# First pair of cached sequences compressed one sequence at a time in a hybrid attention decoder step

## Chip, cores and metric

The kernel runs on one core of one Trainium2 chip. The metric is the device time of one execution in microseconds; of several runs the median counts.

## The reference, cut to what matters

The program is one step of a one-layer decoder: adaLN conditioning, one input projection, forgetting attention beside native sparse attention, a gated merge, an output projection and an MLP. The change lies in the first stage, where the raw keys and values of eight cached sequences (2048 tokens each, in pages of 128 tokens that a page table names) are compressed. What is computed there:

```python
def compress_blocks(x, pos, w1, w2):
    b, n = x.shape[:2]
    n_chunk = n // CMP_STRIDE                        # 16
    xc = x[:, :n_chunk * CMP_STRIDE].reshape(b, n_chunk, CMP_STRIDE, NSA_GROUPS, HEAD_DIM)
    ...
    lead = jnp.einsum('bncgd,cdh->bngh', xc + pos[0], w1[0])
    trail = jnp.einsum('bncgd,cdh->bngh', xc + pos[1], w1[1])
    return jnp.einsum('bngh,hd->bngd', jax.nn.silu(lead[:, :-1] + trail[:, 1:]), w2)

nsa_all = jnp.concatenate([gather_pages(nsa_pool, page_table), pm['nsa_rows']], axis=1)
kc, vc, c_end = compressed_kv(nsa_all[:, :, 0], nsa_all[:, :, 1], lp)
mod = jnp.einsum('bd,de->be', jax.nn.silu(c), lp['w_ada']) + lp['b_ada']
h = rms_norm(x, lp['norm1_g']) * (1.0 + sc1) + sh1
```

The conditioning `mod` and the first norm of the 576 new tokens are worked on in the same stage, between the units of the compression.

## The kernel before

**First stage.** Sequences are handled in four pairs. A unit `u` of 32 is one pair (`u // 8`), one group `j` of four taps (`u // 2 % 4`) and k or v (`u % 2`). For each unit there are these steps:

- `cmp_order` (line 115 is the copy): VectorE copies a tap group of each sequence's pages, tile `cpg`, into a tile `ro` of 128 x 1024; three `ro` buffers exist.
- `cmp_taps`, for the first eight units: ScalarE rounds the tap weights `w1rawk`, `w1rawv` to a high part (line 112) and VectorE makes the low part (line 131), into `w1hlk`, `w1hlv`.
- `rows_turn`: TensorE transposes `ro` into a PSUM bank `ct` (line 83), four transposes for each sequence, one bank each, two banks in turn; ScalarE and VectorE split each bank in two steps each into `xh` and `xl`, a ring of two.
- `cmp_hidden`: twelve matmuls of 512 columns (line 77) add into the bank `hid` of k or v.

After eight units of a pair come `cmp_act` (tiles `csx`, `cst`), `cmp_out` (`co`) and `cmp_keys` (`kct`). Other work hangs in lists `todo[u]` behind the units: `ada_silu` and the turned conditioning, the bias (`posb`), the norms of five token tiles (`norm`, then `turned`, tile `nt`), eight products with `w_ada` (tile `ada`), a gather of log forget values (`lfg`), and loads.

**Order.** In this stage the order on TensorE is the order of the program, by a chain of dependencies (`link`). Order on ScalarE and VectorE is chosen by a planner that simulates a timeline; `issue_after(i)` puts the instructions of a block behind instruction `i` in the queue of its engine. `dma` chains the transfers of one issuing engine in program order.

**Loads.** Each page is one transfer of 128 KB with its page number in a register; each of the two `w1` loads of k or v is 512 KB. SyncE's queue carries nearly all: sequence 0 (16 pages), half of sequence 1, sequence 2, a tile of x, half of sequence 3, x, the conditioning vectors, eight small constants, the rest of sequence 3, w2, and then sequences 4 to 7, x and w_ada. ScalarE issues the `w1` loads of k, eight pages of sequence 1 and the `w1` loads of v. The planner was told to place the constants for later stages (`late_constants`) behind unit 8.

**Afterwards** the projection (`z`), prompt attention, sample attention, merge and MLP follow; the change does not touch them.

Of the kernel before, what the change touches and what calls it, by code (L numbers as in the profile page):

```python
# [14 lines left out]
P = 128  # L15
# [30 lines left out]
class Step:  # L46
# [165 lines left out]
    def constants(self):  # L212
# [4 lines left out]
        for i, n in enumerate("kv"):  # L217
            self.dma("sync", pos[16 * i:16 * i + 16], I[f"cmp_pos_{n}"].rearrange("o (j c) d -> (o j) (c d)", c=2))
        self.dma("sync", c("ptT", [P, 1], I32), I["page_table"].rearrange("b (n o) -> (b n) o", o=1))
        self.dma("sync", chan[0:48], I["b_ada"].rearrange("o (j p) -> (o j) p", p=P))  # L220
        self.dma("sync", chan[48:56], I["norm1_g"].rearrange("o (j p) -> (o j) p", p=P))
        self.dma("sync", chan[56:64], I["norm2_g"].rearrange("o (j p) -> (o j) p", p=P))
        for i, n in enumerate(["fox_qn_g", "nsa_qn_g", "nsa_kn_cmp_g"]):
            self.dma("sync", gains[i:i + 1].rearrange("o (a d) -> o a d", a=2),
                                dram(I[n], 0, [[64, 1], [0, 2], [1, 64]]))
# [13 lines left out]
    def late_constants(self):  # L239
# [14 lines left out]
        for i, n in enumerate(["fox_kn_g", "nsa_kn_slc_g", "nsa_kn_win_g"]):  # L254
            self.dma("sync", kgain[:, i, :], dram(I[n], 0, [[0, P], [1, 64]]))
        self.dma("sync", c("bfox", [P, 8]), dram(I["b_fox_f"], 0, [[0, P], [1, 8]]))
# [5 lines left out]
    def ada_start(self):  # L262
# [3 lines left out]
        self.dma("sync", c9[0:1], self.I["c_prompt"].rearrange("o (k c) -> o k c", k=NK))  # L266
        self.dma("sync", c9[1:9], self.I["c_sample"].rearrange("b (k c) -> b k c", k=NK))
# [83 lines left out]
    def cmp_weights(self, pl):  # L351
# [7 lines left out]
        for i in range(2):  # L359
            x = [pl.tile([P, 2, 514], F32R, name=f"x{n}{i}") for n in "hl"]  # L360
            for t in x:
                self.nc.vector.memset(t[:, :, 512:514].bitcast(F32), 0.0)
            self.ring.append(x)

    def cmp_taps(self, u):

        taps = lambda w: w.rearrange("p (a j) h -> p a j h", a=4)[:, :, u // 2]
        w = self.w1[u % 2]
        self.split(taps(w[:, 0]), taps(w[:, 1]), taps(self.w1raw[u % 2]))

    def cmp_second(self):

        self.w2 = []
        for n in "kv":
            w2 = self.keep.tile([P, 64], F32, name=f"w2{n}")
            w2r = self.keep.tile([P, 64], F32, name=f"w2raw{n}")
            self.dma("sync", w2r, self.I[f"cmp_w2_{n}"][0])
            self.ts(w2, w2r, 0.5, None, OP.mult)
            self.w2.append(w2)
# [57 lines left out]
    def cmp_order(self, pl, n):  # L437

        self.ros[n] = []
        for b in (2 * (n // 4), 2 * (n // 4) + 1):  # L440
            o = pl.tile([P, 2, 4, 2, 64], F32, tag="ro", bufs=3, name=f"ro{n}_{b}")
            self.cp(o.rearrange("p h x c d -> p h c x d"),
                    self.cpg[b][:, :, 2 * (n % 4):2 * (n % 4) + 2].rearrange("p h c (x d) -> p h c x d", x=4))
# [1691 lines left out]
```

## Time and profile before

| | |
|---|---|
| three runs | 1268.05, 1271.83, 1272.16 us; median 1271.83 |
| profiled execution | 1268.96 us, span 1267.2 us |
| granted TensorE clock, mean | 0.985 |
| TensorE busy in the span | 94% |
| DMA | 188.09 MB, mean 148 GB/s |
| first transpose of a page (`ct`) | 26.6 us |
| first matmul of `hid` | 35.6 us |
| last matmul of `hid` ends | 190.5 us |

The times of the rows are microseconds from the start of the span. A row of the timeline has start, length, engine, line, operation, output and inputs, count, and in brackets the engine's idle time before it with what ended it. A "q" behind an engine's name means its sequencer, which issues transfers. In the chain of work that ended last a row has start and length.

### The profile page before, as it was taken

What the parts mean: (1) busy time and instruction counts of PE and PEld (TensorE: products, weight loads), DVE (VectorE), ACT (ScalarE), POOL (GpSimd) and SP (SyncE); (2) the same over time, 40 slices, a digit from 0 to 9 for tenths busy, and PEclk for the clock granted to TensorE, in tenths of its full rate; (3) what the DMA queues carried; (4) which work ended last, traced back from release to release, by engine and by line L of the source; (5) the groups of instructions that cost most, each with busy time, mean ns of one, the idle gap of its engine ahead of it and who ended that gap; (6) DMA issues with size and microseconds to landing.
All of it is one profiled execution on the core that took longest, in us unless ns stands there. A gap on an engine that the chain in (4) does not pass through costs nothing.

```text
span 1267.2 us, 24533 instructions
## 1 busy us (share of the span) xinstructions
PE 1192.0 (94%) x9379; PEld 1021.6 (81%) x9379; DVE 707.1 (56%) x1904; ACT 502.4 (40%) x1119; POOL 99.5 (8%) x107
## 2 busy tenths in 40 slices
PE   0899999999999999999999998977999999999998
PEld 0777789999666656666799998977899899898997
DVE  2578676677688856556543434775234344344564
ACT  2344444444777854444432223233323132142230
POOL 0000000000221120000200000002011010010110
PEclk9899999999999999999999999988999999999999
DMA  9577528597695459796762333114223133141212
GB/s 207 167 225 186 166 66 272 180 332 236 184 297 174 111 199 319 243 316 225 167 175 76 85 99 104 31 50 120 65 83 109 44 115 94 40 133 54 81 34 75
DMA packets 177067, 188.09 MB, mean 148 GB/s; under 512 B 16901, under 2 KB 158766, under 8 KB 174774
## 3 DMA queue, kind: packets, MB, share of 16 engines
q1 hardware_dynamic: 168134, 178.13, 46.5%
q0 software_dynamic: 3504, 5.24, 1.6%
q10 hardware_dynamic: 5312, 3.15, 1.1%
q8 instruction: 74, 1.21, 0.4%
q14 instruction: 43, 0.35, 0.1%
HBM read 176.48 MB, written 30.90 MB: 164 GB/s over the span
## 4 chain that ended last, share of the span: by engine, by line
PE 84%; DVE 6%; DMA 4%; ACT 2%; SPq 2%; issue 1%; DVEq 0%; ACTq 0%
PE dn L77 16%; PE up L77 15%; PE z L77 9%; PE mg L77 8%; PE hid L77 5%; PE br L77 4%; PE wo L77 4%; PE ss L77 4%; PE k L83 2%; PE ct L83 2%; SPq L155 2%; PE so L77 2%; PE ada L77 2%; DMA cpg<-in_cache_nsa_kv 1%; PE sp L83 1%
## 5 line engine op out<-in xcount | busy, mean ns | idle before, releaser
L77 PE MATMUL dn<-wdh,u 128*128 128x512 f32 x576 | 181.9, 389 | 0.0
L77 PEld LDWEIGHTS dn<-wdh,u 128*128 128x128 f32 x576 | 107.5, 188 | 21.9
L77 PE MATMUL dn<-wdl,u 128*128 128x512 f32 x320 | 123.6, 389 | 0.0
L77 PE MATMUL z<-winh,h 128*128 128x264 f32 (+1 forms) x576 | 112.7, 289 | 1.9 <-DVE h L720 1.7
L77 PE MATMUL up<-h,wuh 128*128 128x256 f32 x512 | 94.4, 280 | 6.2 <-ACT h L112 6.2
L77 PEld LDWEIGHTS z<-winh,h 128*128 128x128 f32 x576 | 93.1, 192 | 4.0 <-DVE h L720 2.8
L112 ACT ACTIVATE wdh<-wdr 128x1024 fp32r<-128x1024 f32 x32 | 33.1, 1055 | 147.9 <-PE dn L77 127.6
L77 PE MATMUL z<-winl,h 128*128 128x264 f32 (+1 forms) x320 | 88.7, 286 | 0.0
L100 DVE TENSOR_TENSOR acc<-acc,dn 128x512 f32<-128x512 f32 x60 | 40.4, 686 | 86.3 <-PE dn L77 86.3
L131 DVE TENSOR_TENSOR wul<-wur,wuh 128x1024 fp32r<-128x1024 f32 x32 | 49.1, 1541 | 69.6 <-ACT wuh L112 69.6
L77 PEld LDWEIGHTS up<-h,wuh 128*128 128x128 f32 x512 | 81.2, 192 | 6.5 <-ACT h L112 6.5
L77 PE MATMUL up<-h3H,wuh 128*128 128x320 f32 x256 | 80.0, 313 | 5.8 <-ACT wuh L112 5.8
L77 PE MATMUL up<-h3H,wul 128*128 128x320 f32 x256 | 79.5, 311 | 0.3 <-DVE wul L131 0.3
L77 PE MATMUL up<-h3L,wuh 128*128 128x320 f32 x256 | 79.3, 310 | 0.0
L1926 POOL TENSOR_TENSOR u<-u 128x576 f32<-128x576 f32 x32 | 43.6, 1364 | 438.8 <-ACT u L112 433.6
L77 PE MATMUL mg<-hH,wmh 128*128 128x288 f32 x256 | 75.4, 296 | 1.1 <-ACT wmh L112 1.1
L77 PE MATMUL mg<-hH,wml 128*128 128x288 f32 x256 | 75.2, 295 | 0.9 <-DVE wml L131 0.9
L77 PE MATMUL mg<-hL,wmh 128*128 128x288 f32 x256 | 72.7, 295 | 0.0
L77 PE MATMUL up<-h,wul 128*128 128x256 f32 x256 | 71.7, 280 | 0.0
L112 ACT ACTIVATE xh<-ct 128x256 fp32r<-128x256 f32 x128 | 47.5, 385 | 57.9 <-PE ct L83 37.6
L83 PE MATMUL ct<-identF,ro 128*128 128x128 f32 x256 | 37.4, 292 | 35.1 <-DVE ro L115 30.2
L77 PEld LDWEIGHTS dn<-wdl,u 128*128 128x128 f32 x320 | 60.1, 188 | 12.5
(638 smaller groups left out, 2975.9 us busy)
## 6 DMA issues: line engine op xcount, KB each, us to landing
adw<-in_w_ada SPq DMA_DIRECT2D x16, 1024.0 KB
foxD<-in_cache_fox_kv SPq DMA_DIRECT2D x128, 128.0 KB
wur<-in_w_up SPq DMA_DIRECT2D x32, 512.0 KB
wdr<-in_w_down SPq DMA_DIRECT2D x32, 512.0 KB
cpg<-in_cache_nsa_kv SPq DMA_DIRECT2D x120, 128.0 KB
fr<-foxD SPq DMA_DIRECT2D x28, 512.0 KB
sr<-in_cache_nsa_kv SPq DMA_DIRECT2D x112, 128.0 KB
wada<-in_w_ada SPq DMA_DIRECT2D x8, 1024.0 KB
```

What stands on the lines that cost most here:

```text
L77: ins = self.nc.tensor.matmul(out, a, b, start=start, stop=stop, skip_group_check=True)
L83: ins = self.nc.tensor.transpose(out, in_, self.identF[:n, :n])
L100: self.nc.vector.tensor_tensor(out, a, b, op=op)
L112: return self.nc.scalar.activation(out, in_, f, **kw)
L131: self.splits.append((eng or self.nc.vector).tensor_tensor(l, x, h.bitcast(F32), op=OP.subtract).ins)
L155: self.issued[eng] = getattr(self.nc, eng).dma_start(out, in_).ins
L1926: nc.gpsimd.tensor_tensor(u[j], u[j], u[j], op=OP.mult)
```

## The change

- ScalarE's eight pages are those of sequence 0 (its second half); SyncE loads the other eight, then all of sequence 1, 2 and 3. A one-element Tanh on ScalarE at the start brings its table load there.
- The first two sequences are compressed by themselves: units 0 to 7 are sequence 0, units 8 to 15 sequence 1, both with 256 columns in `cmp_hidden` and one bank in `rows_turn`; units 16 to 39 are pairs 1 to 3 as before. All later work in `todo` moves by eight units.
- The small loads (constants, conditioning vectors) go to GpSimd's queue. Constants for later stages are no longer held back.
- In the first 16 units the copies of `cmp_order`, and the tap splits, are pinned right behind the splits of the unit before (`behind`). Norms start two units ahead of their transposes, not one; `ada_silu`, `stage_logf` and the halving of `w2`, now in place, are pinned too.

```diff
-        self.dma("sync", c("ptT", [P, 1], I32), I["page_table"].rearrange("b (n o) -> (b n) o", o=1))
+        self.dma("gpsimd", c("ptT", [P, 1], I32), I["page_table"].rearrange("b (n o) -> (b n) o", o=1))
...
-        self.dma("sync", c9[1:9], self.I["c_sample"].rearrange("b (k c) -> b k c", k=NK))
+        self.dma("gpsimd", c9[1:9], self.I["c_sample"].rearrange("b (k c) -> b k c", k=NK))
...
-                self.nc.vector.memset(t[:, :, 512:514].bitcast(F32), 0.0)
+                for c in (256, 512):
+                    self.nc.vector.memset(t[:, :, c:c + 2].bitcast(F32), 0.0)
...
     def rows_turn(self, u):
-        n, kv = u // 2, u % 2
+        _, bs, j, kv = self.units[u]
         xh, xl = self.ring[u % 2]
-        for s in range(2):
+        for b in bs:
+            s = b % 2
...
     def cmp_hidden(self, u):
+        c0, w = 256 * (bs[0] % 2), 256 * len(bs)
...
-            for w, x in three((wh, wl), self.ring[u % 2]):
-                self.mm(self.hid[i][kv], w[:, 4 * a + j, :], x[:, a % 2, a // 2:a // 2 + 512], n == 0, n == 47)
+            for y, x in three((wh, wl), self.ring[u % 2]):
+                self.mm(self.hid[i][kv][:, c0:c0 + w], y[:, 4 * a + j, :], x[:, a % 2, c0 + a // 2:c0 + a // 2 + w],
+                        n == 0, n == 47)
...
-        def late():
-            with self.tc.issue_after(self.splits[-1]):
-                self.late_constants()
+        def behind():
+            both = ExitStack()
+            for i in (self.last_high, self.splits[-1]):
+                both.enter_context(self.tc.issue_after(i))
+            return both
+
+        def pinned(f):
+            def g():
+                with behind():
+                    f()
+            return g
...
+        self.units = [(b // 2, bs, j, kv) for b, bs in ((0, (0,)), (1, (1,)), (2, (2, 3)), (4, (4, 5)), (6, (6, 7)))
+                      for j in range(4) for kv in range(2)]
...
-        self.cmp_pages("sync", 0)
-        self.cmp_pages("scalar", 1, slice(0, 8))
+        warm = self.small.tile([P, 1], F32, tag="warm", bufs=1, name="warm")
+        nc.vector.memset(warm, 0.0)
+        self.act(warm, warm, AF.Tanh)
+        self.cmp_pages("sync", 0, slice(0, 8))
+        self.cmp_pages("scalar", 0, slice(8, 16))
         self.cmp_raw(pe, 1)
-        self.cmp_pages("sync", 1, slice(8, 16))
+        self.cmp_pages("sync", 1)
         self.cmp_weights(pl)
+        self.ada_start()
+        self.constants()
+        self.late_constants()
         self.cmp_pages("sync", 2)
         load_x()
-        self.cmp_pages("sync", 3, slice(0, 8))
+        self.cmp_pages("sync", 3)
         load_x()
-        self.ada_start()
-        self.constants()
-        self.cmp_pages("sync", 3, slice(8, 16))
         self.cmp_second()
...
-        for k, u in enumerate((4, 6, 9, 11, 15)):
-            todo[u - 1] += [lambda k=k: norm(k)]
+        for k, u in enumerate((12, 14, 17, 19, 23)):
+            todo[u - 2] += [lambda k=k: norm(k)]
             todo[u] += [lambda k=k: turned(k)]
...
-        for u in range(32):
-            if u % 2 == 0 and u // 2 + 1 < 16:
-                self.cmp_order(pl, u // 2 + 1)
+        for u in range(40):
+            if u % 2 == 0 and u + 2 < 40 and u + 2 != 8:
+                with behind() if u + 2 < 16 else nullcontext():
+                    self.cmp_order(pl, u + 2)
             if u + 1 < 8:
-                self.cmp_taps(u + 1)
-            if u + 1 < 32:
+                with behind():
+                    self.cmp_taps(u + 1)
+            if u + 1 < 40:
                 self.rows_turn(u + 1)
+            if u + 2 == 8:
+                with behind():
+                    self.cmp_order(pl, u + 2)
             self.cmp_hidden(u)
```

86 lines of the change are left out of this document (46 added, 40 removed).

## The prediction

> **What bounds the kernel now.** The page comes first: engine shares, and the chain that ended last.
>
> ```profile
> span 1267.2 us, 24533 instructions
> PE 1192.0 (94%) x9379; PEld 1021.6 (81%) x9379; DVE 707.1 (56%) x1904; ACT 502.4 (40%) x1119; POOL 99.5 (8%) x107
> PE 84%; DVE 6%; DMA 4%; ACT 2%; SPq 2%; issue 1%; DVEq 0%; ACTq 0%
> ```
>
> TensorE is busy for 94% of the span and carries 84% of the chain. Where the other 6% lie the table of windows tells, asked by stage: before the first transpose, the units of the first pair (named below), the second pair up to its last, the rest of the stage, and all behind it. Columns: length, then busy time of PE, PEld, DVE, ACT and POOL with counts, clock, DMA share, GB/s.
>
> ```profile
> 0.00:25.85 25.85, 0.00 (x0) 0.00 (x0) 5.20 (x18) 5.67 (x9) 0.52 (x6) 1.00 1.02 218
> 25.85:77.75 51.90, 42.63 (x263) 35.38 (x264) 30.36 (x90) 18.85 (x46) 1.21 (x1) 0.93 0.58 168
> 77.75:120.10 42.35, 38.64 (x240) 30.61 (x238) 32.49 (x131) 20.76 (x50) 0.00 (x0) 0.96 0.84 223
> 120.10:190.47 70.37, 70.37 (x457) 55.85 (x457) 50.54 (x152) 32.17 (x79) 0.98 (x1) 1.00 0.39 120
> 190.47:1267.20 1076.73, 1040.37 (x8424) 899.75 (x8423) 588.53 (x1514) 425.01 (x938) 96.78 (x99) 0.99 0.47 145
> ```
>
> TensorE does nothing for 25.85 us, is idle for 9.3 of the next 51.9 and 3.7 of the next 42.35, and from 120 us to the end of the stage it is never idle. Everything the change touches lies in the first 190 us. Behind that the work is the same and hangs on TensorE, so what the stage ends earlier, the kernel ends earlier. The timeline shows what the early idle time waits for.
>
> ```profile
> 2.94 37.80 SPq L155 DMA_DIRECT2D cpg<-in_cache_nsa_kv  x40
> 14.52 1.28 ACT L112 ACT_TABLE_LOAD   x1 [14.52 <-DMA cpg<-in_cache_nsa_kv]
> 22.46 2.19 ACT L112 ACTIVATE w1hlv<-w1rawv 128x512 fp32r<-128x512 f32 x4 [4.46 <-DMA w1rawv<-in_cmp_w_v]
> 25.85 0.69 DVE L115 COPY ro<-cpg 128x1024 f32<-128x1024 f32 x1 [0.82 <-DMA cpg<-in_cache_nsa_kv]
> 30.58 1.30 DVE L115 COPY ro<-cpg 128x1024 f32<-128x1024 f32 x2 [1.11 <-DMA cpg<-in_cache_nsa_kv]
> 35.58 1.20 PE L77 MATMUL hid<-xh,w1hlk 128*128 128x512 f32 x2
> 52.12 1.05 ACT L112 ACTIVATE adw<-adw 9x1024 f32<-9x1024 f32 x1 [2.52 <-DMA adw<-in_c_sample]
> 55.03 1.94 PE L83 MATMUL ct<-identF,ro 128*128 128x128 f32 x8 [3.30 <-DVE xl L131]
> ```
>
> Sequence 0 is complete at 25.85 and sequence 1 at about 30.6; only then can the first pair's hidden product start, at 35.58. At 52 us ScalarE stands in front of the small load of c_sample, queued on SyncE behind 48 pages, and TensorE goes without work for 3.30 us.
>
> **The change, part by part.** A unit here is one tap group j of one of k and v for a pair: eight transposes, the splits, twelve matmuls. The first pair's 8 units become 16 of half the width.
>
> *Pages.* ScalarE's eight pages now belong to sequence 0, as SyncE's first eight do.
>
> ```profile
> L155 ACTq DMA_DIRECT2D cpg<-in_cache_nsa_kv x8: 546/546/671, 3.0 to 12.3; - x8
> 9.83 4.88 DMA cpg<-in_cache_nsa_kv
> 14.72 7.20 DMA cpg<-in_cache_nsa_kv
> ```
>
> The second kind of row is from the chain: 4.88 to 7.20 us from a page's issue to its landing. ScalarE issues its last page at 12.3, so sequence 0 is complete at 17.2 to 19.5. Counted in bytes, the 1 MB of k weights and 2 MB of pages take 14.5 us at 218 GB/s, which lies below that. I take 17.5, near the shorter lag since fewer pages are under way by then, 8.3 us earlier than now. Sequence 1's pages all come from SyncE; the bytes up to its end are the same, so about 30 us as now, when sequence 0 is not yet worked off. The fifteen small loads move from SyncE to GpSimd's queue, idle here; the nearest row prices an issue:
>
> ```profile
> 536.31 0.99 POOL L155 DMA_DIRECT2D hH<-hfd  x1 [76.56 <-DVE DH L100]
> ```
>
> That is 15 x 0.99 = 15 us of GpSimd, done by 20 us, needed from about 45 us on: nothing, unless they hold up the pages (0 to 1.5 us, my estimate for under 1,000 short packets over 16 engines). SyncE is rid of them, so pages 2 to 4 come no later. The early table load takes 1.28 us from ScalarE where it would otherwise issue or wait; it may delay its pages by up to 0.5 us and brings the first split forward.
>
> *Prices of a half unit.* First full clock, then the low one, then a product of near 256 columns (all from the chain), then the groups.
>
> ```profile
> 123.90 0.87 PE ct L83 x8
> 121.12 2.78 PE hid L77 x12
> 56.97 4.59 PE hid L77 x12
> 244.83 13.76 PE z L77 x112
> L131 DVE TENSOR_TENSOR xl<-ct,xh 128x256 fp32r<-128x256 f32 x128 | 50.2, 419 | 13.9 <-ACT xh L112 11.1
> L112 ACT ACTIVATE xh<-ct 128x256 fp32r<-128x256 f32 x128 | 47.5, 385 | 57.9 <-PE ct L83 37.6 <-DVE xl L131 18.0
> L115 DVE COPY ro<-cpg 128x1024 f32<-128x1024 f32 x32 | 21.1, 691 | 16.1 <-PE ct L83 14.0 <-DMA cpg<-in_cache_nsa_kv 1.9
> L131 DVE TENSOR_TENSOR w1hlv<-w1rawv,w1hlv 128x512 fp32r<-128x512 f32 x4 | 2.6, 686 | 4.2 <-ACT w1hlv L112 4.2
> ```
>
> A 264-column matmul is 13.76/112 = 0.123 us, so twelve of 256 are 1.43 us against half of 2.78 = 1.39: doubling the number of weight loads costs 16 x 0.04 = 0.6 us in all. With four transposes (0.44) a half unit is 1.87 us of TensorE at full clock and about 3.3 (half of 4.59, plus 1.0) at the low one. The split of a half unit is four steps in turn on one bank (ScalarE waits for VectorE and the other way round in the rows): 2 x (0.385 + 0.419) = 1.6 us. For sequence 0 VectorE also has the low half of the taps (0.69), now pinned between two units where all eight had been done before TensorE started, and every second unit a copy (0.69). In VectorE's order that makes 2.0 us a unit without and 2.7 with the copy, 2.4 in the mean, so sequence 0 runs at VectorE's pace, and sequence 1, without taps, at TensorE's.
>
> *The new course.* Copy at 17.5, transposes to 19.3, split to 21.0, product of unit 0 at the low clock to 23.6. Unit 1 needs the v weights, which ScalarE's queue still brings behind its pages, at 22.46: taps and split end at 25, product at 27.6. Unit 2, still slow, ends at 31, and five units of 2.4 us bring sequence 0 to 43. Ten slow microseconds are my choice after the rows: from 55.03 the clock stayed low to 60.81 (both windows stand under the first rival), and the units have gaps. The Trainium skill ("TensorE: Matmul & The Clock Gate", section Part 1: The HAM clock gate) gives about 3.4 us of sustained work before the full clock. By that rule one or two units less would be slow, at 3.3 - 1.87 = 1.4 us each, and the sum 1.4 to 2.8 us larger; the trace needed 5.8 us, the first half of them with stops, and I keep to it. Sequence 1 has 8 x 1.87 = 15 us of transposes and products, and the conditioning, bias and two norms that move in:
>
> ```profile
> 66.50 0.64 PE L83 MATMUL bc<-identF,adw 9*128 9x9 f32 x8
> 67.20 1.95 PE posb L77 x64
> 86.36 0.76 DVE x L104
> 53.21 1.21 DVE L109 SCALAR_TENSOR_TENSOR adw<-adw 9x1024 f32<-9x1024 f32 x1 [3.10 <-ACT adw L112]
> ```
>
> On TensorE that is 2.0 for the bias, about 1.2 for the small transposes and 2 x 0.87 for the norms': 20 us. On VectorE 16 x 0.42 + 4 x 0.69 + 1.2, two norms of some thirteen 0.16 us steps and 0.76, and four 0.69 us copies and products: 19 us. Both are close, so I add 3 us for hand-overs: 23, and sequence 1 ends at 66. Now the first pair ends at 77.75. **First part of the sum: -11.7 us** (ends: -16, at 19 us for sequence 1 and no loss at the start; -5, at 2.7 us a unit for sequence 0, pages at 19.5 and 26 us for sequence 1).
>
> *Behind the first pair.* The constants (small VectorE steps such as triU's below) leave the place, at 82 us, where they now stand in front of a norm, and norms start two units ahead instead of one.
>
> ```profile
> 82.37 0.22 DVE L104 TENSOR_SCALAR triU<-jp 128x128 f32<-128x128 int32 x1
> 88.27 1.86 PE ada L77 x16
> 100.95 1.00 PE ada L77 x16
> PE nt L83 <- DVE x L104: 3.7, 3, 2.0
> ```
>
> The last row is from TensorE's waits between 78 and 190 us (us in total, times, longest): 3.7 us, all of the idle time there. Behind the 2 us stop the clock is low for a while: 0.9 us on the sixteen ada matmuls, 1.86 against 1.00, and about as much, 0.8, on the eight transposes behind them. So 5.4 us are to be had; **I take -3**, since VectorE has the same norms to do (ends -5.4 and 0). *Edits with one answer.* The pins are an order in a queue and no new semaphore. On ScalarE silu stands behind unit 9's splits and in front of unit 10's; it waits for c_sample, which is there by 20 us, 25 us ahead: nothing. The gather of log forget values and its store keep their distance to the second pair, on GpSimd and SyncE. Four more small memsets run in VectorE's idle first microseconds, and halving w2 in place moves two small steps: nothing. w_ada's first loads go from unit 5 to 12 and 14, four half units ahead of their use, and on SyncE no longer stand behind the pages of sequence 5: nothing. From 120 us on TensorE is full now; the stage keeps its remaining work, and there is nothing to gain: 0. If the pages or w_ada came late for it, that would be the third rival.
>
> The sum is -11.7 - 3 = -14.7, say -14.5. The profiled execution took 1268.96 us, its span plus 1.8; it becomes 1254.5. It lies 2.9 below the median of 1271.83, which becomes 1257.3. I forecast **1256**.
>
> **The rivals.**
>
> *1. The thin units keep TensorE slow (slower).* At the low clock a half unit is 3.3 us; 16 of them, twice the 4.9 us of other products and the 3 us of hand-overs, from 21 us on, end at 21 + 53 + 10 + 3 = 87, 9 us behind the present 77.75; less the 3 us behind it, the kernel is 6 us slower: 1277. It decides at a mean of 2.9 us a unit, (77.75 + 3 - 21 - 10 - 3)/16, which the low clock passes and the full one does not. Here are stretches as long as the shortest one between two changes of the clock in the records (3.41 us):
>
> ```profile
> 53.98:57.40 3.42, 2.37 (x10) 2.31 (x11) 2.66 (x11) 1.49 (x4) 1.21 (x1) 0.50 0.18 40
> 57.40:60.81 3.41, 3.41 (x9) 2.64 (x9) 3.20 (x15) 0.82 (x3) 0.00 (x0) 0.50 0.60 194
> 337.29:340.70 3.41, 2.16 (x28) 1.46 (x26) 2.93 (x14) 2.22 (x7) 0.74 (x1) 1.00 0.75 202
> ```
>
> For it: a stretch 69% busy (53.98) did not lift the clock, one of 100% (57.40) did. Against it: at the low clock a half unit takes longer than VectorE's 2.4 us, so TensorE is full and the clock rises; once high, 63% busy (337.29) kept it, and my units are 78%. The Trainium skill has this rule ("TensorE: Matmul & The Clock Gate", section A second HAM failure mode: psum-queue depth-cycling): frequent short idle times between groups of matmuls can make the clock swing. The stretch at 337 us does not bear it out. Chance 0.05.
>
> *2. No overlap between half units (slower).* If transposes, split and product of a unit run one behind the other, a unit is 0.44 + 1.6 + 1.43 = 3.5, for sequence 0 with taps and copy 5.1: 18 + 41 + 28 + 5 = 92, 14 later, less 3: 1281. For it: the waits between ScalarE and VectorE above. Against it: the next transposes stand ahead of each product and two banks take turns. Chance 0.06.
>
> *3. The head start is given back.* Pages or w_ada for later pairs come when they came, TensorE waits, and the stage ends where it does: 1271, within 0.3%. Against it: the DMA engines moved 168 and 120 GB/s in two of the stretches above where 223 were reached in a third, and SyncE loses fifteen issues. Chance 0.07.
>
> *4. Pages are hardly earlier.* If GpSimd's short transfers and the weights hold sequence 0 until 23 to 25 us, about 6 us of the gain go: 1262. Nothing in the rows needs it beyond the 1.5 us above; the queues' shares of the engines are not shown. Chance 0.13.
>
> **How the numbers follow.** The forecast has 0.69, its own range -8 to -20: 1250 to 1263. Faster: 0.69 + 0.13 = 0.82; same: 0.07 (0.3%, about 4 us, is what can be told from no change); slower: 0.05 + 0.06 = 0.11. The range of 1246 to 1268 takes the bounds of both parts (-16 - 5.4 and -5 - 0 against 1268 to 1271.8) and rival 4.
>
> **What would show it.** Right: first copy near 17.5, first product near 21, granted clock at full by 34, the last product of the stage ending near 176, sequence 1's last product near 66, no idle TensorE on c_sample, the norm's 3.7 us mostly gone. Wrong: TensorE idle over 1 us per half unit, the copy behind 22, w1hlv's taps holding the splits, or TensorE waiting on wada or cpg behind 80 us.

## The result, and the profile after

The changed kernel takes 1274.47 us, median of twelve runs (1269.12 to 1275.96), against 1269.31 us for the kernel before beside it: a ratio of 1.0034, 95% interval 1.0023 to 1.0046. It is slower by some 4 us, where the forecast was 13 to 16 us faster. The profiled execution took 1273.0 us, its span plus 1.8. Three executions in the experiments (1951.56, 1958.39 and 2352.22 us) fell in a slower state, and the ratios leave them out.

First the page of the changed kernel: span, TensorE, and its share of the chain that ended last.

```profile
span 1271.2 us, 24732 instructions
PE 1200.3 (94%) x9475; PEld 1035.6 (81%) x9475; DVE 707.3 (56%) x1909; ACT 502.1 (39%) x1120; POOL 107.3 (8%) x122
PE 85%; DVE 5%; DMA 5%; SPq 2%; ACT 2%; issue 1%; DVEq 0%; ACTq 0%
```

TensorE is still the bound. The table of windows of the same kernel, cut at its own events (first copy of a page, the stop of TensorE in the first pair, end of the stage; columns as in the prediction), shows where the idle time now lies.

```profile
0.00:20.29 20.29, 0.00 (x0) 0.00 (x0) 2.44 (x36) 2.12 (x3) 8.68 (x21) 1.00 0.98 195
20.29:57.30 37.01, 34.24 (x306) 32.41 (x306) 25.49 (x65) 17.04 (x41) 0.00 (x0) 1.00 0.64 179
57.30:93.00 35.70, 22.09 (x114) 19.01 (x116) 16.91 (x57) 11.16 (x26) 0.00 (x0) 0.76 0.71 205
93.00:120.00 27.00, 27.00 (x179) 22.16 (x167) 22.21 (x84) 13.71 (x34) 0.00 (x0) 1.00 0.84 229
120.00:191.08 71.08, 70.69 (x465) 56.20 (x464) 51.39 (x156) 32.84 (x81) 2.19 (x2) 1.00 0.38 114
```

The head start is real: TensorE works from 21 us and is 93% busy up to 57.3. Then it is idle for 13.6 of 35.7 us, at a mean clock of 0.76, and everything is given back. The stage ends at 191.5 instead of 190.5. TensorE's waits between 18 and 190 us (us in total, times, longest) and the rows of the timeline around them name the stops:

```profile
PE ct L83 <- DVE ro L115: 22.5, 2, 21.0
PE hid L77 <- DVE xl L131: 5.5, 1, 5.5
PE hid L77 <- ACT csx L112: 4.8, 1, 4.8
PE nt L83 <- DVE x L104: 3.3, 1, 3.3
```

```profile
20.29 0.69 DVE L115 COPY ro<-cpg 128x1024 f32<-128x1024 f32 x1 [16.69 <-DMA cpg<-in_cache_nsa_kv]
57.16 0.40 PE L77 MATMUL hid<-xh,w1hlv 128*128 128x256 f32 x2
61.93 0.69 DVE L115 COPY ro<-cpg 128x1024 f32<-128x1024 f32 x1 [6.11 <-DMA cpg<-in_cache_nsa_kv]
62.62 0.41 DVE L131 TENSOR_TENSOR xl<-ct,xh 128x256 fp32r<-128x256 f32 x1
63.09 0.58 PE L77 MATMUL hid<-xl,w1hlv 128*128 128x256 f32 x1 [5.53 <-DVE xl L131]
63.49 1.06 ACT L112 ACTIVATE sq<-x 128x1024 bf16<-128x1024 f32 x1 [6.04 <-DMA x<-in_x_prompt]
64.11 0.63 PE L77 MATMUL hid<-xh,w1hlv 128*128 128x256 f32 x2
71.43 1.97 PE L83 MATMUL nt<-identF,x 128*128 128x128 f32 x8 [3.28 <-DVE x L104]
83.60 1.06 ACT L112 ACTIVATE sq<-x 128x1024 bf16<-128x1024 f32 x1 [4.28 <-DMA x<-in_x_prompt]
85.92 1.22 PE L77 MATMUL hid<-xh,w1hlv 128*128 128x512 f32 x2 [4.80 <-ACT csx L112]
```

The stops in turn. In unit 13 (the expectations below count from one and call it unit 14) TensorE stops after five matmuls because the low half of the split, `xl`, is missing. `xl` is missing because VectorE stands in front of a copy that the second pair needs later, of a tap group of sequence 3, whose pages have not all landed. ScalarE stands at the same time in front of the Square of the second norm, for its tile of x; from that norm the stop at 71.43 follows. The third norm waits for its tile until 83.6, and behind its Square in ScalarE's queue stand the splits and `csx`. After each stop comes a stretch at the low clock: right behind the first one two `hid` matmuls take 0.63 us (64.11), where two took 0.40 at 57.16.

All three loads come over SyncE's queue. Its issues of x in the kernel before, then in the changed kernel (the first three of each), with rows of pages between them, and under each what SyncE's issues of pages waited for in the first 45 us (us in total, times, longest):

```profile
40.79 0.59 SPq L155 DMA_DIRECT2D x<-in_x_prompt  x1
42.15 5.61 SPq L155 DMA_DIRECT2D cpg<-in_cache_nsa_kv  x8
47.81 0.58 SPq L155 DMA_DIRECT2D x<-in_x_prompt  x1
63.38 0.35 SPq L155 DMA_DIRECT2D x<-in_x_prompt  x1
SPq L155 <- DMA cpg<-in_cache_nsa_kv: 6.0, 7, 2.4
```

```profile
45.54 0.59 SPq L155 DMA_DIRECT2D x<-in_x_prompt  x1
46.91 12.63 SPq L155 DMA_DIRECT2D cpg<-in_cache_nsa_kv  x16
59.59 0.58 SPq L155 DMA_DIRECT2D x<-in_x_prompt  x1
75.13 0.52 SPq L155 DMA_DIRECT2D x<-in_x_prompt  x1
SPq L155 <- DMA cpg<-in_cache_nsa_kv: 9.8, 7, 3.0
```

Work that starts 13 us earlier is fed by loads that come 12 us *later*. Of these 12 us, 4.8 are there at the first tile already: forty pages stand ahead of it in both kernels, but in the changed one SyncE's issues waited 9.8 us for earlier pages to land, not 6.0. For the second tile, 7 more come from the order: it now stands behind all sixteen pages of sequence 3 (12.63 us of issuing) instead of eight. The third stands behind the sixteen pages of sequence 4 and a `w_ada` load, where it had stood ahead of them. For these loads it does not hold that all work in `todo` moves by eight units. The pages of sequence 4 move by four, and x changes places with them:

```diff
-        for b, u in ((4, 4), (5, 6), (6, 12), (7, 14)):
-            todo[u] += [load_x] * (b < 6) + [lambda b=b: self.cmp_tile(pe, b), lambda b=b: self.cmp_pages("sync", b)]
...
+        todo[8] += [pages(4)]
+        todo[12] += [wada(0), load_x]
+        todo[14] += [pages(5), load_x, wada(1)]
```

There is a second loss, far from the change. From the up and down matmuls of the MLP to the end the two kernels run the same 2376 matmuls; the windows of before and after:

```profile
865.00:1267.20 402.20, 397.08 (x2376) 361.32 (x2376) 173.89 (x231) 113.60 (x199) 43.60 (x32) 0.99 0.27 78
```

```profile
866.00:1271.20 405.20, 400.39 (x2376) 364.67 (x2376) 173.93 (x231) 113.65 (x198) 43.27 (x32) 0.99 0.25 78
```

TensorE is busy 3.3 us longer. The pages of the two kernels show the group that grew most, before and after (busy us, mean ns of one):

```profile
L77 PE MATMUL up<-h,wuh 128*128 128x256 f32 x512 | 94.4, 280 | 6.2 <-ACT h L112 6.2
L77 PE MATMUL up<-h,wuh 128*128 128x256 f32 x512 | 97.7, 284 | 4.7 <-ACT h L112 4.7
```

Taken from the start times, the 256-column matmuls of `up` (these and 256 of the low part) start every 118.9 ns instead of 113.6; 768 of them make 4.1 us. The other kinds in the MLP keep their pace (medians of 147 and 227 ns).

### The profile page after: what moved, and what is told of

Same layout as the page of the kernel before. It is cut to its first block, busy times and chain, and to the rows that moved or that the text cites. A ratio compares the mean times of both kernels' runs of the same rounds, so it can differ in the third digit from the quotient of the medians.

```text
span 1271.2 us, 24732 instructions
## 1 busy us (share of the span) xinstructions
PE 1200.3 (94%) x9475; PEld 1035.6 (81%) x9475; DVE 707.3 (56%) x1909; ACT 502.1 (39%) x1120; POOL 107.3 (8%) x122
## 3 DMA queue, kind: packets, MB, share of 16 engines
q1 hardware_dynamic: 167154, 177.94, 45.5%
## 4 chain that ended last, share of the span: by engine, by line
PE 85%; DVE 5%; DMA 5%; SPq 2%; ACT 2%; issue 1%; DVEq 0%; ACTq 0%
PE dn L77 16%; PE up L77 15%; PE z L77 8%; PE mg L77 8%; PE hid L77 5%; PE wo L77 4%; PE br L77 4%; PE ss L77 4%; SPq L155 2%; PE k L83 2%; DMA cpg<-in_cache_nsa_kv 2%; PE ct L83 2%; PE so L77 2%; PE ada L77 2%; PE sp L83 1%
## 5 line engine op out<-in xcount | busy, mean ns | idle before, releaser
L77 PE MATMUL z<-winh,h 128*128 128x264 f32 (+1 forms) x576 | 112.7, 289 | 1.9 <-DVE h L751 1.7
L77 PE MATMUL up<-h,wuh 128*128 128x256 f32 x512 | 97.7, 284 | 4.7 <-ACT h L112 4.7
L77 PE MATMUL z<-winl,h 128*128 128x264 f32 (+1 forms) x320 | 88.6, 286 | 0.0
L131 DVE TENSOR_TENSOR wdl<-wdr,wdh 128x1024 fp32r<-128x1024 f32 x32 | 38.5, 1220 | 50.2 <-ACT wdh L112 50.2
```

Source lines behind the costliest of these rows:

```text
L77: ins = self.nc.tensor.matmul(out, a, b, start=start, stop=stop, skip_group_check=True)
L131: self.splits.append((eng or self.nc.vector).tensor_tensor(l, x, h.bitcast(F32), op=OP.subtract).ins)
```

## The experiments

Ratios are to the kernel before, run on the same chip beside each; its medians were 1270.12, 1269.45, 1269.38 and 1269.27 us in the four groups.

A trace is one execution, and executions scatter. Five kernels below differ from the changed kernel by a pad alone, and their traces end the first stage at 186.9 to 189.7 us, against 191.5 in the changed kernel's. Behind the stage, where the work is the same, the traces with `up` at 113.6 ns take 1073.9 to 1079.7 us. So a few us between two traces say nothing by themselves; the ratios compare kernels, the traces name the stops.

**The MLP: a matter of addresses?** The change drops two tiles of 256 bytes each per partition (`w2k`, `w2v`, since `w2` is halved in place) and adds one of 32, so every later tile lies 480 bytes lower. One kernel puts the 480 bytes back; another takes them out of the kernel before.

```diff
 # the changed kernel, in cmp_second
+        pad = self.keep.tile([P, 120], F32, name="pad")
+        self.nc.vector.memset(pad, 0.0)
```

> The changed kernel with a 480-byte tile added to the pool that w2 left, so that all later tiles lie where they lay before; the order of work is the same. Theory 'supply and addresses': the MLP slowed because the 256-column matmuls of up took 0.119 instead of 0.114 us (768 of them, 4 us), and this goes back with the addresses: 3 to 4 us less than the changed kernel, ratio to before 0.999 to 1.002. Rival 'drift': the MLP's 3 us are chance of single profiles or follow from the time at which the stage ends; then the ratio stays at 1.003 and the spacing at 0.119.

```diff
 # the kernel before, in cmp_second (and a tile of 32 bytes added)
-            w2 = self.keep.tile([P, 64], F32, name=f"w2{n}")
...
-            self.ts(w2, w2r, 0.5, None, OP.mult)
-            self.w2.append(w2)
+            self.ts(w2r, w2r, 0.5, None, OP.mult)
+            self.w2.append(w2r)
```

> The kernel before, with nothing changed but 480 bytes less in front of all later tiles (w2 halved in place, and a 32-byte tile). Theory 'supply and addresses': 256-column matmuls of up at 0.119 us, 3 to 4 us slower than before, ratio 1.002 to 1.004. Rival 'drift': ratio 1.000, spacing 0.114.

The window of the MLP, first of the changed kernel with the pad, then of the shifted kernel before:

```profile
867.40:1269.40 402.00, 397.17 (x2375) 361.42 (x2374) 173.56 (x231) 113.36 (x198) 43.51 (x32) 0.99 0.26 78
```

```profile
863.80:1265.00 401.20, 400.49 (x2376) 364.75 (x2376) 172.72 (x230) 113.73 (x198) 43.24 (x32) 1.00 0.26 78
```

The loss goes with the bytes, in both directions: with the pad 1271.76 us, ratio 1.0008 (0.9992 to 1.0023); the shifted kernel before 1273.27 us, 1.0029 (1.0016 to 1.0043). So 3 of the 4 to 5 us are this, and the rest of the change is worth nothing measurable.

**Which property of the address?** Pads of other sizes in the changed kernel.

> The changed kernel with a tile of 32 bytes only ahead of the later tiles, which then lie 448 bytes below where the kernel before has them, at 92128 instead of 92096 for the first block of up weights. If what counts is the place within 64 bytes (32 above a multiple of 64 in the fast kernels, on a multiple in the slow ones), the upper matmuls of 256 columns start every 113.6 ns and the kernel is like the one with the pad of 480 bytes: ratio 0.999 to 1.002. Rival (the old absolute address or the distance to another tile counts): 119 ns and ratio 1.0025 to 1.0045, as the changed kernel.

> The changed kernel with a tile of 96 bytes ahead of the later tiles; the first block of up weights lies at 92192, which is 32 above a multiple of 128 as in the fast kernels (92576), but 160 off within 256. Period 128: the upper matmuls of 256 columns start every 113.6 ns. Period 256 or more: 118 to 119.5 ns.

> The changed kernel with a tile of 224 bytes; the first block of up weights lies at 92320, the same place within 256 (and 128) bytes as in the fast kernels. Period 128 or 256: 113.6 ns. A longer period, or the distance to one certain tile: 118 to 119.5 ns.

> The changed kernel with a tile of 64 bytes; the first block of up weights lies at 92160, a multiple of 128, a place within 128 bytes that no run has had so far (fast 32, slow 64 and 96). If 32 is the only fast place: 118 to 119.5 ns; if the two of four places nearest to it are fast: 113.6 ns.

| first block of up weights at | within 256 | `up<-h,wuh` starts every |
|---|---|---|
| 92576 (before; pad of 480) | 160 | 113.6 ns |
| 92320 (pad of 224) | 160 | 113.6 ns |
| 92096 (the change; before, shifted) | 192 | 118.9 ns |
| 92608 (GpSimd's pages, below) | 192 | 118.9 ns |
| 92128 (pad of 32) | 224 | 118.7 ns |
| 92160 (pad of 64) | 0 | 119.9 ns |
| 92192 (pad of 96) | 32 | 117.8 ns |

My first rule, a place within 64 bytes, fell with the pad of 32 (1273.17 us, 1.0026, 1.0009 to 1.0043), and a period of 128 with the pad of 96 (single run, 1274.41 us). A place within 256 bytes fits all rows; with the pad of 224 the single run took 1269.52 us, with that of 64 it took 1274.19. These three times are of one run each, so it is the pace in their traces that decides. The places 64, 96 and 128 were not tried, and since all later tiles move together, which tile's place counts is open.

**The order of loads.** The third and fourth tile of x ahead of the pages and `w_ada` they stand behind:

```diff
-        todo[8] += [pages(4)]
-        todo[12] += [wada(0), load_x]
-        todo[14] += [pages(5), load_x, wada(1)]
+        todo[12] += [load_x, pages(4), wada(0)]
+        todo[14] += [load_x, pages(5), wada(1)]
```

> The changed kernel with the third and fourth tile of x loaded in front of the pages of sequences 4 and 5 and of w_ada, not behind them. Theory 'supply': the Square of the third norm no longer stands on ScalarE in front of a load that comes at 83 us; the 4.8 us that TensorE waits for ScalarE's csx and the low clock behind it go: 5 to 8 us less than the changed kernel, ratio to before 0.997 to 1.000. Rival 'thin units' (the loss lies in half-width units and their hand-overs): no more than 1 us less.

> The changed kernel with two edits together: a 480-byte tile that puts every later tile back at its old address, and the loads of x2 and x3 issued on SyncE ahead of the pages and w_ada they stood behind. Address theory and supply theory add up: addresses gave 3.2 us back, x earlier about 4 (the wait for csx is gone). So the upper matmuls of 256 columns start every 113.6 ns, the stage ends 3 to 7 us before the kernel before, and the ratio to the kernel before is 0.995 to 0.998. Rival (thin units: what is won by one removed stop is lost in the clock of half units, so the order of loads can't matter): ratio 1.000 to 1.001, as the pad alone gave.

Without the pad 1269.79 us, 1.0004 (0.9981 to 1.0026), at the edge of the 0.997 to 1.000 expected; with it 1268.77 us, 0.9990 (0.9969 to 1.0011). TensorE's waits, with the pad:

```profile
PE hid L77 <- DVE xl L131: 4.5, 1, 4.5
PE nt L83 <- DVE x L104: 3.3, 1, 3.3
PE ada L77 <- DMA wada<-in_w_ada: 3.2, 1, 3.2
```

The wait on `csx` is gone. In its place TensorE reaches the second `w_ada` tile before that has landed: it is issued at 88.6, behind the pages of sequence 5, and wanted at 93.7, where the changed kernel used it at 102.8. Against the pad alone (1.0008) early x brings 2.3 us, which the intervals don't separate from nothing, and the 0.995 to 0.998 expected was missed: the direction fits the supply theory, the size was overrated.

**The copy of sequence 3 out of VectorE's way.**

```diff
-                    self.cmp_order(pl, u + 2)
+                    self.cmp_order(pl, u + 2, (2,) if u == 14 else None)
...
+            if u == 14:
+                with behind():
+                    self.cmp_order(pl, 16, (3,))
```

> The kernel with pad and early x, and in it the copy of the pages of sequence 3 for the second pair put behind the splits of unit 15, so that VectorE does not stand in front of unit 14's and 15's splits until those pages have landed. In-order theory: the stop inside unit 14 (5.5 us in the changed kernel, 4.3 with early x) is VectorE's place in its order, so it goes to under 1.5 us; but the pair's next unit still needs the pages (complete near 61.6), so only the work of units 14 and 15 that is left, 2 to 4 us, moves under the wait: 1 to 4 us less than the kernel with pad and early x (ratio of the two 0.997 to 0.999). Rival (pages rule: unit 16 needs sequence 3 whatever stands before it): the stop moves to unit 16's transposes with nearly the same length, 0 to 1 us less.

1266.99 us, 0.9982 (0.9963 to 1.0001): 1.8 us less than without it, which the intervals don't separate. The wait on `xl` vanished, and in its place, at nearly the same time, stands another:

```profile
62.70 1.06 ACT L112 ACTIVATE sq<-x 128x1024 bf16<-128x1024 f32 x1 [5.53 <-DMA x<-in_x_prompt]
64.17 0.79 PE L77 MATMUL hid<-xh,w1hlk 128*128 128x256 f32 x2 [5.27 <-ACT xh L112]
```

Neither expectation had this: the Square of the second norm, in ScalarE's order, held the high half of the next split exactly as the copy had held the low half on VectorE. Its tile of x lies on SyncE right behind sequence 3.

**More issuing engines.** GpSimd issues the second halves of sequences 1 and 3 right behind its small loads; then, in another kernel, those of 2 and 3, and only once the v weights of unit 1 are there.

```diff
-        self.cmp_pages("sync", 1)
+        self.cmp_pages("sync", 1, slice(0, 8))
...
+        self.cmp_pages("gpsimd", 1, slice(8, 16))
...
-        self.cmp_pages("sync", 3)
+        self.cmp_pages("sync", 3, slice(0, 8))
+        self.cmp_pages("gpsimd", 3, slice(8, 16))
```

> The changed kernel with the second halves of sequences 1 and 3 (16 pages) issued by GpSimd, behind the small loads. Theory 'supply' (SyncE issues a page in 0.72 us and sequence 3 is complete only at 61.6 us; VectorE's copy of it stands in front of the splits of units 14 and 15): sequence 3 is complete near 50, TensorE no longer stops from 57.3 to 63.1, and the queue behind is 11 us earlier: 8 to 14 us less than the changed kernel, ratio 0.992 to 0.997. Rival 'DMA engines full' (the engines, not the issue, set the pace): sequence 3 near 60, at most 2 us. Rival 'thin units': stop gone, but no gain.

```profile
36.52 0.63 ACT L112 ACTIVATE w1hlv<-w1rawv 128x512 fp32r<-128x512 f32 x1 [12.17 <-DMA w1rawv<-in_cmp_w_v]
37.20 1.31 PE L77 MATMUL hid<-xh,w1hlv 128*128 128x256 f32 x2 [11.53 <-ACT w1hlv L112]
```

A miss: 1276.43 us, 1.0056 (1.0035 to 1.0077). The stop in unit 13 went, but the second load of v weights, which in the changed kernel lands 10.1 us after its issue, took 21.5 with GpSimd's pages on the way as well, and unit 1 waited 11.5 us. What each queue moved from 20 to 25.6 us, in the changed kernel and in this one (packets, MB, share of the 16 engines; q1 is SyncE's, q10 ScalarE's with the v weights, q0 GpSimd's):

```profile
q1 hardware_dynamic: 852, 0.78, 63.5%
q10 hardware_dynamic: 1104, 0.55, 47.5%
```

```profile
q0 software_dynamic: 276, 0.76, 59.3%
q10 hardware_dynamic: 506, 0.25, 26.7%
q1 hardware_dynamic: 303, 0.28, 24.1%
```

The sum is about the same, 1.33 and 1.29 MB, and the shares add up to over 100% in both. So the engines were full, and what GpSimd's queue got, the two others lost. In this stretch the rival of full engines was right. SyncE lost too: the last of its pages of sequence 3 was issued at 56.2, and the 50 us expected for the whole sequence were missed. The loss agrees with what the Trainium skill states ("DMA: Bandwidth & Descriptors", section Queues, rings and completion order): each DMA engine takes packets in turn from the queues that have work for it.

```diff
 # with the pad and early x
+            if u == 0:
+                mark = self.small.tile([P, 1], F32, tag="mark", bufs=1, name="mark")
+                self.issued["gpsimd"] = nc.gpsimd.tensor_copy(mark, self.w1[1][:, 1, 0, 0:1].bitcast(F32)).ins
+                self.cmp_pages("gpsimd", 2, slice(8, 16))
+                self.cmp_pages("gpsimd", 3, slice(8, 16))
```

> The kernel with pad and early x, and in it the second halves of sequences 2 and 3 issued on GpSimd's queue, begun only when the v weights of unit 1 have landed, so that they do not slow those as they did when they began at once. Supply theory (SyncE's pace of 0.72 us a page sets when sequence 3 is complete): sequence 3 complete at 50 to 55 instead of 61.6, no stop at unit 14, x1 and x2 earlier too, the stage 4 to 9 us earlier than with pad and early x, ratio to the kernel before 0.990 to 0.994. Rival (the 16 engines are full with these bytes, 0.64 to 0.71 busy in this stretch): sequence 3 stays near 60, time as with pad and early x within 1 us. Second rival (two queues slow the rest as before): a wait of over 5 us for another load shows up in TensorE's waits.

1266.51 us, 0.9974 (0.9961 to 0.9987): 3 us faster than before, though `mark`, one more 32-byte tile, had moved the later tiles and its `up` matmuls went at 118.9 ns. The pages of sequence 3 were issued by 50.4 us (59.5 in the change), the copy of them at 55.8 did not wait, no wait over 3 us is left behind the first copy, and the stage of this trace ends at 180.8. Still the 0.990 to 0.994 expected was missed; the address explains 0.0025 of the gap. The windows from 26 to 50 us, of the change and of this kernel, and this kernel's issue of the first half of sequence 3:

```profile
26.00:50.00 24.00, 22.07 (x196) 20.98 (x198) 16.67 (x38) 11.44 (x28) 0.00 (x0) 1.00 0.58 173
```

```profile
26.00:50.00 24.00, 21.64 (x201) 20.37 (x203) 16.80 (x38) 11.15 (x28) 9.04 (x17) 1.00 0.96 229
40.00 10.39 SPq L155 DMA_DIRECT2D cpg<-in_cache_nsa_kv  x8
```

In the change the engines were not full, 0.58 busy. With a second issuer they are, at 0.96, and SyncE's own eight pages now take 10.4 us to issue, since the issues wait for earlier loads to land. The room was worth a third more GB/s, no more.

```diff
 # early x, GpSimd's pages and the split copy together, and
+        pad = self.keep.tile([P, 112], F32, name="pad")
```

> The version of all that helped: early x, the second halves of sequences 2 and 3 on GpSimd's queue behind the v weights, the copy of sequence 3 behind unit 15's splits, and a pad that puts the later tiles back at the very address of the kernel before (in the kernel with GpSimd's pages a 32-byte tile had moved them again, and its upper matmuls of 256 columns went at 119 ns). Address theory: 113.6 ns and 3.2 us less than the kernel with GpSimd's pages; supply theory: the stop at unit 14 stays gone, the split copy adds 0 to 1 us. Ratio to the kernel before 0.994 to 0.9965 (1261.5 to 1265). Rival (the 119 ns come from traffic on the queues, not from an address): 119 ns again and 0.997 to 0.998.

Together, with the address put right: 1263.55 us, 0.9953 (0.9935 to 0.9972, five executions), the fastest kernel of this study, 6 us faster than the kernel before and, by the two ratios, some 10 faster than the change. `up` went at 113.6 ns.

**The other direction.** The fifteen small loads back on SyncE, at their new place ahead of sequence 2.

```diff
-        self.dma("gpsimd", c9[1:9], self.I["c_sample"].rearrange("b (k c) -> b k c", k=NK))
+        self.dma("sync", c9[1:9], self.I["c_sample"].rearrange("b (k c) -> b k c", k=NK))
 # and the fourteen others alike
```

> The changed kernel with its fifteen small loads back on SyncE's queue, at the place where they now are issued, behind the pages of sequence 1 and ahead of those of sequence 2. If GpSimd's small loads are what brought sequence 0 to 20.1 instead of the 17.5 that I forecast, its first copy now begins at 17 to 18.5; if it is the sharing of 16 engines between pages and weights, it stays at 20. SyncE then issues the pages of sequences 2 and 3 some 8 to 10 us later (15 issues of 0.55 us), and by the supply theory the stop at unit 14 grows from 5.5 to 11 to 15 us and the kernel is 3 to 8 us slower than the changed kernel (1277 to 1282, ratio to before 1.006 to 1.010). Rival (supply does not bind, the thin units do): within 1 us of the changed kernel.

```profile
16.87 0.69 DVE L115 COPY ro<-cpg 128x1024 f32<-128x1024 f32 x1 [13.27 <-DMA cpg<-in_cache_nsa_kv]
```

```profile
PE nt L83 <- DVE x L104: 15.4, 2, 8.2
PE hid L77 <- ACT csx L112: 6.1, 1, 6.1
```

Both parts held: the first copy begins at 16.87 (in the kernels with small loads on GpSimd at 18.6 to 20.3), so they did slow sequence 0; and the kernel takes 1279.91 us, 1.0083 (1.0069 to 1.0097), by the two ratios 6 us more than the change, although it *starts* 3 us earlier. SyncE's later issues come 5 us later, not the 8 to 10 that I expected: the tiles of x at 51.0 and 64.4 us instead of 45.5 and 59.6. The stops stand at the norms, behind these tiles, rather than in unit 13, whose stop was expected to grow. This is the plainest evidence that the supply sets the end of the stage.

**What the one-by-one start is worth.** The first pair compressed together again, first with the rest of the change as it is (and the pad), then with the better supply.

```diff
-        self.units = [(b // 2, bs, j, kv) for b, bs in ((0, (0,)), (1, (1,)), (2, (2, 3)), (4, (4, 5)), (6, (6, 7)))
+        self.units = [(b // 2, bs, j, kv) for b, bs in ((0, (0, 1)), (2, (2, 3)), (4, (4, 5)), (6, (6, 7)))
 # and all places in todo moved back by eight units
```

> The changed kernel (with the 480-byte pad) with its first pair compressed together again, eight units of full width, the rest of the change as it is. Supply theory: the order and pace of the pages and x sets when the second pair can run, so the 8 half units that start at 20 us win nothing in the end; first pair done at 69 to 74, no stop for sequence 3, stage end within 4 us of the changed kernel's (187 to 192), ratio to the kernel before 0.997 to 1.002, the same as with the pad alone (1.0008). Rival (the head start is worth what the sum gave it, and something else costs): first pair done at 74 to 78, 5 to 12 us slower than with the pad alone, ratio 1.005 to 1.010. Second rival (the thin units cost): 4 us or more faster than the pad alone, ratio below 0.998.

> The version with early x, GpSimd's pages and the address put back, but the first pair compressed together as in the kernel before. Now the pages of sequences 2 and 3 no longer bind (complete by 53), so the first pair's own end should: it starts at 31 instead of 20 and takes 8 units of about 3.7 us at full clock, bias and norms, ending at 66 to 71 where one by one it ended at 57 to 59. Supply theory: the head start is worth something only here, 4 to 9 us slower than the version of all that helped (ratio between 0.998 and 1.003 to the kernel before). Rival (the head start is worth nothing at any supply, since w_ada, x and the pages of sequences 4 and 5 bind next): within 2 us of it.

```diff
 # of the two with the better supply, from the first to the second
-        todo[6] += [load_x, pages(4), wada(0), load_x, pages(5), wada(1)]
+        todo[4] += [load_x, pages(4), wada(0)]
+        todo[6] += [load_x, pages(5), wada(1)]
```

> The version with early x, GpSimd's pages and the address put back, with the first pair compressed together, and now with x, pages and w_ada of the third pair asked for in the order and at the units of the kernel before (behind unit 4 and unit 6). The wait for w_ada of 7.4 us goes. If the one-by-one start is worth its head start where supply does not bind: first pair done at 66 to 71, and 4 to 8 us slower than the version of all that helped (ratio to the kernel before 0.998 to 1.002). Rival (it is worth nothing, w_ada was all of the difference): within 2 us of that version, ratio 0.994 to 0.997.

(In this last kernel the first two norms also start at units 3 and 5, not 5 and 6.) As the change stands: 1272.91 us, 1.0020 (1.0006 to 1.0034), against 1.0008 (0.9992 to 1.0023) one by one. The first pair ended at 73.1, as the supply theory had it; the stage at 194.3, later than the 187 to 192 expected, after a stop of 8.4 us that was not expected. It is once more the third tile of x, issued at 73.2 and waited for until 81.7. So at this supply a head start of 16 us (first `hid` at 22.2 against 38.5) is worth some 1.5 us, which the intervals don't separate from nothing. With the better supply: 1274.18 us, 1.0037 (1.0023 to 1.0052), and with the third pair's loads in the old order 1271.49, 1.0016 (1.0003 to 1.0029), which by the ratios is 8 us behind the version of all that helped. The first pair ended at 72.8 and 73.1, not at the 66 to 71 expected, and one by one at 68.2, not at the 57 to 59 that the expectation has. But the wait I meant to take away stayed:

```profile
PE ada L77 <- DMA wada<-in_w_ada: 6.6, 2, 4.9
```

Sequence 4's pages can only be asked for when a page buffer is free: from 58.0 us on one by one, from 66.7 in this run, where they also stand behind a tile of x whose buffer the first norm frees. So the 8 us are an earlier start and earlier buffers together; I can't part the two.

The start of the first `hid` matmul of the second pair's fifth unit, from each timeline, sums it up (us):

| kernel | first `hid` | fifth unit of second pair |
|---|---|---|
| before | 35.6 | 103.6 |
| the change | 22.7 | 105.6 |
| with pad of 480 bytes | 22.2 | 103.4 |
| with pads of 32, 64, 96, 224 | 21.1 to 22.5 | 100.8 to 103.0 |
| early x, no pad | 22.3 | 97.6 |
| pad, early x | 22.0 | 102.1 |
| pad, early x, copy of sequence 3 behind | 21.8 | 97.6 |
| pad, early x, GpSimd's pages | 22.0 | 94.8 |
| version of all that helped | 21.0 | 95.8 |
| small loads on SyncE | 19.2 | 108.5 |
| pairs, rest as the change | 38.5 | 108.0 |
| pairs, better supply, old order | 38.3 | 105.5 |

Each figure is of one execution, and those that differ by a pad alone lie 5 us apart. While SyncE issues alone, the fifth unit doesn't follow the start: the earliest start, 19.2, has the latest fifth unit, 108.5. It follows the loads. Where GpSimd issues pages too, one by one is 10 us ahead of pairs, an earlier start and earlier buffers together.

## Why the prediction was wrong

**Pages (term of 8.3 us).** I put the first copy at 17.5 and gave GpSimd's small loads 0 to 1.5 us; it came at 20.29. The run with them on SyncE had 16.87, so they cost 1.8 to 3.4 us. Of the 8.3 us, 5.6 were left: a third of the term went the way of the fourth rival (pages hardly earlier).

**Prices of a half unit.** Right. Units 8 and 9 take 1.9 us each by their start times (forecast 1.87), and units 3 to 7 take 2.4 in the mean, as forecast. That sequence 0 ended at 42.6 (forecast 43) is part luck: it began 2.8 us late and made that up in a shorter slow stretch. The thin units did not keep TensorE slow: the first rival is out. The clock was better than I chose: not ten slow microseconds but about six, from the first transposes at 21.04 to the matmuls on `xl`, which take 0.41 us each up to 25.72 and 0.28 from 27.22 on. (The windows give 1.00 as the granted clock even there; the lengths of the matmuls show it.) The 5.8 us that the trace of before had needed were right, and I had counted more. The rule of the Trainium skill that I had weighed and put aside ("TensorE: Matmul & The Clock Gate", section Part 1: The HAM clock gate, about 3.4 us of sustained work) was nearer than my ten.

**The end of the first pair (term of -11.7).** Forecast 66, measured 76.3, against 77.75 before. Of the 11.7 us, 1.4 came. Sequence 1 was to take 23 us for 20 of work and took 33.7. The stops at 57 and 68 us are 8.8 us of that, the half-speed stretches behind them about 4 (estimated as half of 63.1 to 67.8 and of 71.4 to 74.6); without them it is 21. The work was priced well. What failed is that this term had no line for loads beyond sequences 0 and 1.

**Behind the first pair (-3), and the step that failed.** From the end of the first pair to the end of the stage the change took 115.1 us against 112.7: +2.4, not -3. The step that failed, here and in the term above, is the price of nothing that I set for the later loads. I wrote that SyncE "is rid of them, so pages 2 to 4 come no later". For sequence 2 that was false: its pages are issued by 45.5, not by 40.7. For sequences 3 and 4 it was true, and beside the point: work that starts 13 us earlier needs them 13 us earlier, and from 26 us on SyncE issues one page each 0.72 us. Of `w_ada` I wrote that it no longer stands behind the pages of sequence 5. The rows show the reverse, before at 77.8 and ahead of them, after with its second load at 91.2 and behind them; no wait on it came of that in the change. Of the x tiles, moved *behind* the pages of sequences 3 and 4 by the same lines of the diff, I did not ask at all, and they came 12 us later. Most of this could have been read from the issue rows of x in the trace of before, 47.81 and 63.38, and the pages now ahead of each; the 4.8 us by which the first forty pages came later could not.

**The third rival.** "The head start is given back: 1271", at a chance of 0.07, describes what happened; with the address loss taken out the measurement is 1271.76, beside 1270.12 for the kernel before. My argument against it was the rate: 168 and 120 GB/s where 223 were reached. But from 26 us on the queue was not short of bandwidth (0.58 of the engines busy up to 50), it was short of issues, and an average rate over the engines does not show that. The chain of waits of the kernel before did not show it either, since there the late start hid it.

**"Halving w2 in place moves two small steps: nothing."** Two small steps cost nothing; the two tiles that are gone cost 3 us in the MLP, behind 866 us. Nothing in the rows of before could have priced this, but with it the forecast of the third rival would have been 1274 to 1275.

**Ends.** Of the signs I had named as right, the first copy (20.29), the last product of the first pair (76.3), the norm's wait (3.3 us left) and the end of the stage (191 against 176) failed; the first product came at 22.7 instead of 21; the full clock by 34 and no idle time on c_sample held. None of the signs of being wrong appeared either: the list had waits on `wada` and `cpg` behind 80 us, and not the tiles of x.

## What to carry to other kernels

A head start is worth what the *next* loads allow: before pricing it, write down for each later load when it is issued, what now stands ahead of it in its queue, and when the earlier work will ask for it. In engines that work in order, an instruction placed ahead for a later unit (a copy, a norm's Square) becomes the stop of the present one as soon as its data is late, and moving one away only uncovers the next until the load itself comes earlier. And when a change adds or drops a small tile, compare the pace of the same matmuls far from the change.

## What the runs showed of the hardware

- 256-column matmuls in `up` start every 113.6 ns or every 117.8 to 119.9 ns, by the place of the tiles within 256 bytes of SBUF: 3 us of this kernel by the two runs that moved nothing else. `up` matmuls of the other form (147 ns) and `dn` (227 ns) did not change.
- A page of 128 KB with its number in a register takes SyncE 0.72 us from issue to issue (sixteen in 12.63 us, with a stop to fetch page numbers). From 26 to 50 us that, not the 16 DMA engines (0.58 busy, 173 GB/s), was the limit in the change. With half of the pages of sequences 2 and 3 issued by GpSimd the engines were 0.96 busy at 229 GB/s and became the limit themselves.
- With GpSimd's pages on the way as well, a 512 KB load on ScalarE's queue landed 21.5 us after its issue instead of 10.1; from 20 to 25.6 us its queue moved 0.25 MB instead of 0.55, at the same sum over all queues.
